# MLP of a two-layer decoder trunk: the first quarter of the first matrix as seven block products too, with its block sums and three token sums on GpSimd

## The chip, the cores and the metric

The kernel runs on one core of one Trainium2 chip. The metric is device time in microseconds (us) of one execution; lower is better. TensorE (PE in the profile) multiplies matrices, VectorE (DVE) and ScalarE (ACT) do elementwise work and read the matmuls' results, GpSimd (POOL) does elementwise work on SBUF and issues some DMAs, and SyncE (SP) issues the other DMAs.

## What is computed

Two layers, each a token mixer (attention and an mLSTM) followed by an MLP. Only the MLP is touched by the change:

```python
u = jax.nn.relu(rmsnorm(x, norm_ffn) @ w_ff1)
return x + (u * u) @ w_ff2
```

x has 512 tokens of 1024 features, w_ff1 is 1024 x 4096, w_ff2 is 4096 x 1024, all float32. The MLP is computed once per layer, so the change acts twice.

## The kernel before, in words

**Numbers in two parts.** TensorE multiplies fp32r numbers. Each float32 operand is split into a high part (`hi`, a copy on ScalarE that rounds) and a low part (`lo`, a subtraction on VectorE of high from the whole). A product of two such operands takes three matmuls (`mm3`, L184): high by high, high by low, low by high. So each block of weights costs one 128x1024 copy on ScalarE (`two_parts`, L1212) and one 128x1024 subtraction on VectorE (L1213) before TensorE can use it. The names are wh and wl for weights, uh and ul for the hidden values, i for the normed tokens, t for sums of them. Four pairs of wh and wl tiles rotate (pool `spl`), so a split also waits until TensorE has finished with the block four halves earlier.

**The four quarters.** w_ff1 is taken in four quarters of 1024 columns (`part` 0 to 3), and w_ff2 in the four matching quarters of 1024 rows. The second matrix (`second_slots`) is done in all quarters as seven block products: a 2x2 block product of matrices with seven instead of eight multiplications, at the price of sums of blocks. The first matrix is done so in quarters 1 to 3 (`first_slots`, L1363). There the tokens' side has four quads: j says which half of the features, t which half of the tokens. The products use quads as they are or sums of quads, t1 to t4, which `t_steps` (L1325) makes once per layer: b12 (whole numbers of one quad), t1 (two sums, in a second scratch tile), t2 (two sums, in place on t1's), t3 (two, in place on b12's), t4 (two, in place on t2's). Each of t1 to t4 is then split in two parts. In before all of these sums are on VectorE (L1332 to L1357). On the weights' side the sums are made by DMAs that add to what is there (`more`, L1382), which GpSimd issues.

**Quarter 0 of the first matrix** is done plainly, by `First` (L1274): four column groups q of 256 columns, each with eight k tiles, two column tiles and three matmuls of 128x512 over all tokens. Groups 0 and 1 run first, woven together, k tiles 4 to 7 before 0 to 3, since the mixer finishes the features of k tiles 4 to 7 first. In between come what `late` holds: the transposes and norm copies (`Norm.turn`, L270: four transposes into an `aux` bank, a copy on ScalarE at L180, an instruction on VectorE at L181) of k tiles 0 to 3. Groups 2 and 3 are the first two `Slot`s.

**The slots.** After that the work is a list of slots of two halves each. `go(i)` prepares the weights up to four halves ahead (`prepare(i + 4)`: loads, splits, sums), then runs half i on TensorE, then reads its banks (`done`). `extra` (L1638) hangs the steps b12, t1, t2, t3, t4 behind halves 1, 3, 5, 9, 13. In quarters 1 to 3, a product of the first matrix is 48 matmuls of 128x256, one of the second matrix 24 of 128x512. The results of a product are first copied from the bank (`first_read`, ScalarE) and later products are added (`then_read`, VectorE, then two activations on ScalarE).

**What sets the order.** The Python order gives each engine's queue a start, but a scheduler reorders within it; what is marked `tc.high_priority()` (loads, weight splits, bank reads) goes ahead of other ready work. `ask` (L1236) makes all loads go out behind the first four. Every engine then runs its own queue strictly in the order that is built, and an instruction that waits holds up those behind it. Raw weight blocks lie in eleven tiles (`raws`) that are handed out in turn; `drop` gives one back.

Of the kernel before, what the change touches and what calls it, by code (L numbers as in the profile page):

```python
# [33 lines left out]
def hybrid_kernel(ctx, tc, x, norm_mix, w_in, att_q_norm, att_k_norm, att_sinks, m_gate_bias,  # L34
# [63 lines left out]
    def f32(ap):  # L98
        return ap.bitcast(F32)
# [1086 lines left out]
    def mlp(l, norm, late, phase):  # L1186
# [24 lines left out]
        def two_parts(src, hi, lo):  # L1211
            sc.activation(hi, src, AF.Copy)  # L1212
            ve.tensor_tensor(lo, src, f32(hi), op=ALU.subtract)  # L1213
            return hi, lo
# [59 lines left out]
        class First:  # L1274


            def __init__(self, q, which="f"):
                self.q, self.which, self.w = q, which, {}

            def load(self, h):  # L1280
                with tc.high_priority():
                    r = raw([P, 4, H])
                    ask(r, w_ff1[l, 4 * h * P:4 * (h + 1) * P, H * self.q:H * (self.q + 1)]
                        .rearrange("(k p) n -> p k n", p=P))
                self.w[h] = w_split(r)
                drop(r)

            def step(self, k, order=range(KT)):
                if k == order[0]:
                    self.ps = banks(self.which)  # L1290
                hi, lo = self.w[k // 4]
                for m in range(2):
                    c = slice(m * P, (m + 1) * P)
                    mm3(self.ps[:, m, :], hi[:, k % 4, c], lo[:, k % 4, c], acts[k][0], acts[k][1],
                        k == order[0], k == order[-1])

            def evac(self, u):
                i, m = self.q // 2, 2 * (self.q % 2)
                with tc.high_priority():
                    for t in range(2):  # L1300
                        dst = u[t, i][:, m:m + 2, :]
                        sc.activation(dst, self.ps[:, :, H * t:H * (t + 1)], AF.Relu)
                        sc.activation(dst, dst, AF.Square)

# [5 lines left out]

        def first_slot(q, u, which):
            f = First(q, which)
            return Slot(f.load, lambda h: [f.step(k) for k in range(4 * h, 4 * h + 4)], lambda: f.evac(u))

# [10 lines left out]
        def t_steps():  # L1325
# [37 lines left out]
        def first_slots(part, new):  # L1363
# [20 lines left out]
            def w2(h):  # L1384
                load(a12, h, 0, 1)

                def then():
                    load(s, h, 1, 0)
                    more(s, h, 1, 1)

                return a12[h], then, a12[h]

            def w1(h):
                load(a11, h, 0, 0)
                return a11[h], lambda: None, a11[h]
# [22 lines left out]
            def fresh_y():  # L1418
                ys[:] = [aux(), aux()]
# [3 lines left out]
            def product_(y, fresh, w, moving, done):  # L1423
# [9 lines left out]
                def run(h):  # L1433
                    if h == 0 and fresh:
                        if y:
                            fresh_y()
# [44 lines left out]
            return {  # L1481
                2: product_(True, True, w2, lambda: quad(1, 0), lambda: first_read((0, 0), True)),
                1: product_(False, True, w1, lambda: quad(0, 0), lambda: then_read((0, 0), False, ALU.add)),
                5: product_(True, True, w5, lambda: t_parts[1], done5),
                6: product_(False, False, w6, lambda: t_parts[2], lambda: first_read((1, 0), False)),
                7: product_(False, False, w7, lambda: t_parts[3], done7),
                3: product_(True, False, w3, lambda: quad(1, 1), lambda: then_read((1, 0), True, ALU.add)),
                4: product_(True, True, w4, lambda: t_parts[4], lambda: then_read((0, 1), True, ALU.add)),
# [131 lines left out]
        f01, turned = [First(0, "f"), First(1, "y")], [4, 5, 6, 7, 0, 1, 2, 3]  # L1620
        for h in (1, 0):
            for f in f01:
                f.load(h)
        weave([(0.5, lambda k=k, f=f: f.step(k, turned)) for k in turned for f in f01], late + [(4.5, factor)])
        for f in f01:
            f.evac(us[0])
        slots = [first_slot(2, us[0], "x"), first_slot(3, us[0], "f")]
        for part in range(4):
            p = second_slots(part, us[part])
            if part < 3:  # L1630
# [100 lines left out]
```

## Time and profile before

| | |
|---|---|
| median of 3 runs | 1270.65 us (1270.12 to 1270.93) |
| profiled execution, span from first to last instruction | 1268.6 us |
| granted TensorE clock | 1.00 throughout |
| busy: PE, DVE, ACT, POOL | 1261.9, 1036.7, 794.4, 265.3 us |
| first matrix starts on TensorE, first and second layer | 317.40 and 946.45 us |

The page of the profile shows one execution. Its sections are: busy time of each engine; the span in 40 slices; DMA queues; the chain of work that ended last, followed back from the end; the costliest groups of instructions; DMA issues. Other views list groups of one stretch, instructions in order of time (start, length, engine, line, operation, output<-input, count), the chain in order of time, and busy time of each engine in given stretches (length, then busy time with the number of instructions for PE, PEld, DVE, ACT, POOL, then the granted clock, the DMA share and GB/s). All times in those views count from the span's start.

### The profile page before, as it was taken

The numbers are of one execution on the slowest core, as the hardware profiler recorded it, in microseconds if no ns is written. First come the engines' busy times: TensorE is split into PE (matmuls) and PEld (weight loads), VectorE is DVE, ScalarE is ACT, GpSimd is POOL, SyncE is SP. The second block draws the span as 40 slices with busy tenths as digits, with TensorE's granted clock in tenths as the row PEclk, the third lists the DMA queues.
The fourth block names the chain that finished last, engine by engine and source line by source line (L and its number), as shares of the span: only waits on it lengthen the run. The fifth ranks groups of instructions, "written<-read, shape, count | busy, mean of one in ns | idle before, by whom it ended". The sixth has DMA issues, their size and how long they took to land.

```text
span 1268.6 us, 19228 instructions
## 1 busy us (share of the span) xinstructions
PE 1261.9 (99%) x6882; PEld 1089.8 (86%) x6882; DVE 1036.7 (82%) x1646; ACT 794.4 (63%) x1403; POOL 265.3 (21%) x361
## 2 busy tenths in 40 slices
PE   9999999999999999999999999999999999999998
PEld 7888888888889999999888888888888899999987
DVE  4788988688787887969957989876878879879697
ACT  5578578546555666656554885876466556565563
POOL 4513131020003031130115041310300121302210
PEclk9999999999999999999999999999999999999999
DMA  5425473476669798897224345634757697988953
GB/s 159 113 71 155 110 123 99 136 141 148 195 156 216 198 200 208 204 205 205 35 75 117 93 124 117 117 112 129 157 136 198 162 220 201 196 218 189 217 143 99
DMA packets 138927, 193.35 MB, mean 152 GB/s; under 512 B 10568, under 2 KB 79024, under 8 KB 138832
## 3 DMA queue, kind: packets, MB, share of 16 engines
q1 hardware_dynamic: 92992, 129.72, 33.3%
q0 software_dynamic: 45120, 62.00, 30.7%
q8 instruction: 54, 0.88, 0.3%
q10 hardware_dynamic: 720, 0.40, 0.1%
q14 instruction: 41, 0.34, 0.1%
HBM read 188.95 MB, written 2.10 MB: 151 GB/s over the span
## 4 chain that ended last, share of the span: by engine, by line
PE 98%; ACT 1%; DVE 0%; issue 0%; DMA 0%; DVEq 0%; POOL 0%; ACTq 0%; POOLq 0%
PE mm L47 79%; PE aux L47 16%; PE aux L52 3%; DMA w<-in_w_in_dram 0%; DVE a L962 0%; ACT wh L167 0%; ACT a L751 0%; ACT L241 0%; ACT L240 0%; ACT a L947 0%; ACT aux L948 0%; ACT t L177 0%; ACT i L180 0%; DVE t L178 0%; ACT kT L598 0%
## 5 line engine op out<-in xcount | busy, mean ns | idle before, releaser
L47 PE MATMUL mm<-i,wh 128*128 128x512 f32 (+1 forms) x1280 | 353.0, 363 | 0.0
L1212 ACT ACTIVATE wh<-raw 128x1024 fp32r<-128x1024 f32 x212 | 223.2, 1056 | 178.9 <-PE mm L47 90.4
L1213 DVE TENSOR_TENSOR wl<-raw,wh 128x1024 fp32r<-128x1024 f32 x212 | 255.4, 1220 | 80.9 <-ACT wh L1212 80.9
L47 PEld LDWEIGHTS mm<-i,wh 128*128 128x128 f32 x1280 | 221.8, 189 | 29.4
L47 PE MATMUL mm<-i,wl 128*128 128x512 f32 (+1 forms) x640 | 229.2, 359 | 0.0
L47 PE MATMUL mm<-wh,uh 128*128 128x512 f32 x440 | 171.8, 390 | 0.0
L47 PE MATMUL mm<-wl,uh 128*128 128x512 f32 x440 | 171.7, 390 | 0.0
L47 PE MATMUL mm<-wh,ul 128*128 128x512 f32 x440 | 171.2, 389 | 0.0
L1382 POOL DMA_DIRECT2D raw<-in_w_ff_dram x48 | 62.6, 1312 | 381.0 <-DMA raw<-in_w_ff_dram 175.6
L47 PEld LDWEIGHTS mm<-i,wl 128*128 128x128 f32 x640 | 120.9, 189 | 18.6
L167 ACT ACTIVATE wh<-w 128x512 fp32r<-128x512 f32 (+1 forms) x144 | 86.3, 603 | 61.6 <-PE mm L47 45.2
L168 DVE TENSOR_TENSOR wl<-w,wh 128x512 fp32r<-128x512 f32 (+1 forms) x144 | 95.6, 667 | 32.9 <-ACT wh L167 31.2
L47 PE MATMUL mm<-wh,i 128*128 128x512 f32 (+1 forms) x352 | 99.5, 356 | 0.6 <-ACT wh L167 0.6
L47 PEld LDWEIGHTS mm<-wh,ul 128*128 128x128 f32 x440 | 82.6, 188 | 17.5
L1267 DVE SCALAR_TENSOR_TENSOR x<-mm,ms,x 128x512 f32<-128x512 f32 x126 | 90.6, 744 | 8.3 <-PE mm L47 8.3
L47 PEld LDWEIGHTS mm<-wh,uh 128*128 128x128 f32 x440 | 82.8, 188 | 16.0
L47 PEld LDWEIGHTS mm<-wl,uh 128*128 128x128 f32 x440 | 82.8, 188 | 15.6
L1539 POOL DMA_DIRECT2D raw<-in_w_ff_dram x36 | 43.5, 1209 | 150.7 <-DVE wl L1213 126.2
L47 PEld LDWEIGHTS mm<-wh,i 128*128 128x128 f32 x352 | 62.0, 188 | 9.4 <-ACT wh L167 0.8
L47 PE MATMUL aux<-t,wh 128*128 128x256 f32 x384 | 69.5, 283 | 0.0
L47 PE MATMUL aux<-i,wh 128*128 128x256 f32 x384 | 69.5, 283 | 0.0
L47 PE MATMUL mm<-wl,i 128*128 128x512 f32 (+1 forms) x176 | 61.8, 351 | 0.0
(324 smaller groups left out, 2531.8 us busy)
## 6 DMA issues: line engine op xcount, KB each, us to landing
raw<-in_w_ff_dram SPq DMA_DIRECT2D x144, 512.0 KB, 4.9
raw<-in_w_ff_dram POOLq DMA_DIRECT2D x84, 512.0 KB, 8.1
w<-in_w_in_dram SPq DMA_DIRECT2D x112, 256.0 KB, 2.7
a<-in_w_in_dram POOLq DMA_DIRECT2D x32, 256.0 KB, 5.8
qa<-in_w_out_dram POOLq DMA_DIRECT2D x12, 512.0 KB, 6.6
a<-in_w_in_dram SPq DMA_DIRECT2D x16, 256.0 KB, 4.4
w<-in_w_att_branch_dram SPq DMA_DIRECT2D x16, 256.0 KB, 2.9
w<-in_w_m_branch_dram SPq DMA_DIRECT2D x16, 256.0 KB, 2.9
```

The source lines that it names most:

```text
L47: latest[0] = nc.tensor.matmul(*args, **kw)
L52: latest[0] = nc.tensor.transpose(*args)
L167: sc.activation(wh[:, :off], raw[:, :off], AF.Copy)
L168: ve.tensor_tensor(wl[:, :off], raw[:, :off], f32(wh[:, :off]), op=ALU.subtract)
L1212: sc.activation(hi, src, AF.Copy)
L1213: ve.tensor_tensor(lo, src, f32(hi), op=ALU.subtract)
L1267: ve.scalar_tensor_tensor(xh[:, cc], ps[i][:, cc], ms[j][:, b:b + 1], xh[:, cc], op0=ALU.mult, op1=ALU.add)
L1382: gp.dma_start(to[h], src(h, i, j), accum_op=ALU.add)
L1539: gp.dma_start(to[h], src(h, i, j), accum_op=ALU.add)
```

## The change

`First` and `first_slot` go. Quarter 0 becomes seven block products too, and these are the order of the slots now: product 2 of quarter 0, product 2 of quarter 1, then products 1, 5, 6, 7, 3, 4 of quarter 0, then the second matrix of quarter 0 mixed with the rest of quarter 1. In quarter 0 the sums of weight blocks are not made by adding DMAs: four blocks are loaded for each half (a11, a12, b10, b11; one more, a22, later), and GpSimd adds them in place, four sums of 128x1024 for each half: b11 += b10, b10 += a11, a11 += b11, a12 += a11. In the token sums, the two additions each of t2, t3 and t4 go from VectorE to GpSimd. These are plain two-operand sums, so t2 and t4 are made with the other sign, and the split turns it (`minus=True`: scale -1 on ScalarE, a scalar_tensor_tensor on VectorE). b12 and t1 stay on VectorE, and so do all splits. The steps hang behind halves 3 (b12 and t1), 5, 7 and 9 (`sums_at`). The norm copies that `late` holds now come behind halves 0 to 2 (one half counts 1.0), at 1.0, 1.5, 2.0 and 2.5.

```diff
+        def two_parts(src, hi, lo, minus=False):
+            if minus:
+                sc.activation(hi, src, AF.Copy, scale=-1.0)
+                ve.scalar_tensor_tensor(lo, src, -1.0, f32(hi), op0=ALU.mult, op1=ALU.subtract)
...
-        class First:
...
             def t2():
                 d = scratch["b"]
-                ve.scalar_tensor_tensor(d, d, -1.0, h22, op0=ALU.mult, op1=ALU.subtract)
-                ve.tensor_tensor(d, d, l22, op=ALU.subtract)
-                t_parts[2] = two_parts(d, *t_new("t2"))
+                gp.tensor_tensor(d, d, h22, op=ALU.add)
+                gp.tensor_tensor(d, d, l22, op=ALU.add)
+                t_parts[2] = two_parts(d, *t_new("t2"), True)
             def t3():
                 d = scratch["a"]
-                ve.tensor_tensor(d, h22, d, op=ALU.subtract)
-                ve.tensor_tensor(d, d, l22, op=ALU.add)
+                gp.tensor_tensor(d, h22, d, op=ALU.subtract)
+                gp.tensor_tensor(d, d, l22, op=ALU.add)
                 t_parts[3] = two_parts(d, *quad(0, 1))
             def t4():
                 d = scratch["b"]
-                ve.tensor_tensor(d, d, h21, op=ALU.add)
-                ve.tensor_tensor(d, d, l21, op=ALU.add)
-                t_parts[4] = two_parts(d, *t_new("t4"))
+                gp.tensor_tensor(d, d, h21, op=ALU.subtract)
+                gp.tensor_tensor(d, d, l21, op=ALU.subtract)
+                t_parts[4] = two_parts(d, *t_new("t4"), True)
...
+            if part == 0:
+                b10, b11 = ([None] * 2 for _ in range(2))
+                def add(to, h, more_):
+                    with tc.high_priority():
+                        gp.tensor_tensor(to[h], to[h], more_[h], op=ALU.add)
+                def begin(h):
+                    load(b10, h, 1, 0)
+                    load(b11, h, 1, 1)
+                def w2(h):
+                    load(a12, h, 0, 1)
+                    return a12[h], lambda: None
+                def w1(h):
+                    load(a11, h, 0, 0)
+                    def then():
+                        add(b11, h, b10)
+                        add(b10, h, a11)
+                        add(a11, h, b11)
+                    return a11[h], then
+                def w5(h):
+                    return b11[h], lambda: None, b11[h]
+                def w6(h):
+                    return a11[h], lambda: add(a12, h, a11), a11[h]
+                def w7(h):
+                    return b10[h], lambda: None, b10[h]
+                def w3(h):
+                    return a12[h], lambda: None, a12[h]
...
-        f01, turned = [First(0, "f"), First(1, "y")], [4, 5, 6, 7, 0, 1, 2, 3]
...
-        slots = [first_slot(2, us[0], "x"), first_slot(3, us[0], "f")]
+        begin0, f0 = first_slots(0, us[0], {2: "y", 5: "y"})
+        f1 = first_slots(1, us[1], {2: "x"}, begin0)[1]
+        slots = [f0[2], f1[2]] + [f0[n] for n in (1, 5, 6, 7, 3, 4)]
...
-        extra = dict(zip((1, 3, 5, 9, 13), t_steps()))
+        sums_at, sums = {3: 2, 5: 1, 7: 1, 9: 1}, []
...
-        weave(steps, side)
+        weave([(1.0, go) for _, go in steps[:5]], late + [(4.0, factor)])
+        weave(steps[5:], side)
...
-        late = norm.steps(0, 1.5, 0.5)
+        late = norm.steps(0, 1.0, 0.5)
```

The lines of the changed program are 2 to 4 off from those of before (L1212 is L1216, L1213 is L1217). The names in the rows below, for the first layer: i_3583, i_3584 are the high and low parts of the normed tokens of k tiles 4 to 7, i_3765, i_3766 (before: i_3748, i_3749) those of k tiles 0 to 3; raw_3895 (before: raw_3969) is the scratch tile of b12 and t3, raw_3897 (before: raw_4046) that of t1, t2 and t4; t_829, t_830 (before: t_849, t_850) are the two parts of t1. Of the weights, raw_3703 and raw_3709 are a12 of quarter 0 (halves 0 and 1), raw_3725 is the second half of a12 of quarter 1, raw_3721 and raw_3731 are b10, raw_3723 and raw_3733 b11, raw_3769 and raw_3819 a11. aux_3853 (before: aux_3784) is the bank with the last of the four transposes that `late` holds.

VectorE at the start of the MLP, before: the low parts of four weight blocks are done, then come the norm copies, b12, and the low part of a block of column group 2.

```order
L1213 TENSOR_TENSOR wl_3720<-raw_3717,wh_3719 128x1024
L181 SCALAR_TENSOR_TENSOR i_3749<-aux_3743,gcol,i_3748 128x512
L181 SCALAR_TENSOR_TENSOR i_3749<-aux_3758,gcol,i_3748 128x512
L181 SCALAR_TENSOR_TENSOR i_3749<-aux_3771,gcol,i_3748 128x512
L181 SCALAR_TENSOR_TENSOR i_3749<-aux_3784,gcol,i_3748 128x512
L1332 TENSOR_TENSOR raw_3969<-i_3748,i_3749 128x1024
L1213 TENSOR_TENSOR wl_3886<-raw_3883,wh_3885 128x1024
```

And now, at the same place, three blocks ahead of the norm copies and five behind:

```order
L1217 TENSOR_TENSOR wl_3718<-raw_3715,wh_3717 128x1024
L181 SCALAR_TENSOR_TENSOR i_3766<-aux_3760,gcol,i_3765 128x512
L181 SCALAR_TENSOR_TENSOR i_3766<-aux_3805,gcol,i_3765 128x512
L181 SCALAR_TENSOR_TENSOR i_3766<-aux_3812,gcol,i_3765 128x512
L181 SCALAR_TENSOR_TENSOR i_3766<-aux_3853,gcol,i_3765 128x512
L1300 TENSOR_TENSOR raw_3895<-i_3765,i_3766 128x1024
L1217 TENSOR_TENSOR wl_3728<-raw_3725,wh_3727 128x1024
L1217 TENSOR_TENSOR wl_3772<-raw_3769,wh_3771 128x1024
L1217 TENSOR_TENSOR wl_3822<-raw_3819,wh_3821 128x1024
L1217 TENSOR_TENSOR wl_3865<-raw_3723,wh_3864 128x1024
```

The fourth weight block that TensorE needs (wl_3728, second product, second half) moved behind the norm copies and b12; in before the fourth (wl_3720) stood ahead of them.

ScalarE, some way on, before: the high part of t1 (t_849) between weight splits.

```order
L1212 ACTIVATE wh_3891<-raw_3889 128x1024
L240 ACTIVATE nrt_3817<-nv_3813 128x4
L1212 ACTIVATE t_849_4049<-raw_4046 128x1024
L241 ACTIVATE ncol_3816<-nrt_3817 128x4
L1212 ACTIVATE wh_3897<-raw_3895 128x1024
```

And now:

```order
L1216 ACTIVATE wh_3920<-raw_3733 128x1024
L1466 ACTIVATE u_3892<-mm_3828 128x512 x2
L262 ACTIVATE junk,nss_3147<-x_0_89 128x512
L1216 ACTIVATE wh_3949<-raw_3769 128x1024
L1216 ACTIVATE i_3765<-raw_3895 128x4x256
L1216 ACTIVATE t_829_3900<-raw_3897 128x1024
L1216 ACTIVATE wh_3987<-raw_3819 128x1024
```

The high part of t3 (written to i_3765 from raw_3895) moved to the place right before that of t1; in before it stands some twenty rows behind it.

GpSimd, before: the adding DMAs of the mixer's end, and right behind them those of the MLP's weights.

```order
L1145 DMA x_0_87<-st_3365 128x512
L1105 DMA t_3247<-in_w_out_dram 128x512
L1105 DMA t_3262<-in_w_out_dram 128x512
L1382 DMA raw_4015<-in_w_ff_dram 128x4x256
L1382 DMA raw_4059<-in_w_ff_dram 128x4x256
```

And now, from the last of the mixer's DMAs to the second sum of t3:

```order
L1105 DMA t_3262<-in_w_out_dram 128x512
L1390 TENSOR_TENSOR raw_3723<-raw_3723,raw_3721 128x1024
L1390 TENSOR_TENSOR raw_3721<-raw_3721,raw_3769 128x1024
L1390 TENSOR_TENSOR raw_3733<-raw_3733,raw_3731 128x1024
L1390 TENSOR_TENSOR raw_3731<-raw_3731,raw_3819 128x1024
L1390 TENSOR_TENSOR raw_3769<-raw_3769,raw_3723 128x1024
L1390 TENSOR_TENSOR raw_3703<-raw_3703,raw_3769 128x1024
L1390 TENSOR_TENSOR raw_3819<-raw_3819,raw_3733 128x1024
L1390 TENSOR_TENSOR raw_3709<-raw_3709,raw_3819 128x1024
L1317 TENSOR_TENSOR raw_3895<-i_3583,raw_3895 128x1024
L1318 TENSOR_TENSOR raw_3895<-raw_3895,i_3584 128x1024
```

Eight block sums and the two of t3 moved in; the two of t2 and the two of t4 follow, and then the adding DMAs. The second layer has the same rows in the same order.

More of the change, by code (lines that the diff above doesn't have):

```diff
@@ L1385, in w2 @@
                 load(a12, h, 0, 1)
[L1387 to L1391, printed above, removed]
+                return a12[h], lambda: (after_two or begin)(h), a12[h]
+            def begin(h):
+                load(s, h, 1, 0)
+                more(s, h, 1, 1)
             def w1(h):
                 load(a11, h, 0, 0)
-                return a11[h], lambda: None, a11[h]
+                return a11[h], lambda: after_two and begin(h), a11[h]
             def w5(h):
```

76 lines of the change are left out of this document (23 added, 53 removed).

## The prediction

> **What bounds the kernel now.** I read the page first: how busy each engine is, and who owns the chain of work that ended last.
>
> ```profile
> span 1268.6 us, 19228 instructions
> PE 1261.9 (99%) x6882; PEld 1089.8 (86%) x6882; DVE 1036.7 (82%) x1646; ACT 794.4 (63%) x1403; POOL 265.3 (21%) x361
> PE 98%; ACT 1%; DVE 0%; issue 0%; DMA 0%; DVEq 0%; POOL 0%; ACTq 0%; POOLq 0%
> ```
>
> TensorE owns 98% of the chain, so a matmul saved is time saved, and any wait on TensorE is time lost. Next come the chain in order of time around the start of the first MLP and at the same place in the second layer, and engine time by stretch.
>
> ```profile
> 316.64 0.77 PE aux L52 x6
> 317.40 4.10 PE mm L47 x18
> ...
> 326.34 0.44 PE aux L52 x4
> 326.77 40.84 PE mm L47 x180
> 367.62 5.75 PE aux L47 x48
> ...
> 955.80 40.84 PE mm L47 x180
> 996.64 5.75 PE aux L47 x48
> ```
>
> ```profile
> 306.70:367.60 60.90, 60.90 (x286) 50.30 (x284) 44.68 (x52) 38.23 (x62) 2.58 (x2) 1.00 0.63 181
> 367.60:631.00 263.40, 263.40 (x1637) 238.48 (x1636) 224.36 (x225) 159.59 (x164) 53.23 (x44) 1.00 0.81 181
> ```
>
> The MLP's matmuls start at 317.40 and TensorE never waits until 631. VectorE (third pair of numbers in the last two rows) is at 44.68 of 60.90 us in the stage that changes, GpSimd (fifth) at 2.58. Both layers show the same pieces, so I work out the first and double it.
>
> **TensorE's own work.** A 512-wide matmul costs 40.84/180 = 0.2269 us, a 256-wide one 5.75/48 = 0.1198. Per layer the change removes 4 x 8 x 2 x 3 = 192 of the first (43.56 us) and adds 7 x 48 = 336 of the second (40.25). It saves 3.3 us per layer, 6.6 in all, if nothing waits. The transposes stay. I number the new half products 0 to 15 (24 matmuls, 2.88 us each): 0 and 1 are the first quarter's product 2, 2 and 3 the second quarter's, then products 1 (4, 5), 5 (6, 7), 6 (8, 9), 7, 3 and 4.
>
> **Price of GpSimd's sums.** Before has no 128x1024 sum there. The nearest rows are four 128x512 sums in a stretch, in each layer, what VectorE did just before and meanwhile (in order of time), and a smaller product from the groups.
>
> ```profile
> 31.36 4.12 POOL L515 TENSOR_TENSOR t<-a 128x512 f32<-128x512 f32 x4 [7.82 <-ACT a L416]
> 660.19 4.43 POOL L515 TENSOR_TENSOR t<-a 128x512 f32<-128x512 f32 x4 [32.12 <-ACT a L416]
> ```
>
> ```profile
> 30.72 0.86 DVE L304 TENSOR_SCALAR t<-ident,nch 128x128 fp32r<-128x128 f32 x4
> 31.50 4.06 DVE L304 TENSOR_SCALAR t<-ident,ncl 128x128 fp32r<-128x128 f32 x4
> ...
> 659.13 0.43 DVE L168 TENSOR_TENSOR wl<-w,wh 128x264 fp32r<-128x264 f32 x1 [2.29 <-ACT wh L167]
> 661.85 0.67 DVE L168 TENSOR_TENSOR wl<-w,wh 128x264 fp32r<-128x264 f32 x1 [2.29 <-ACT wh L167]
> ```
>
> ```profile
> L547 POOL TENSOR_TENSOR rp<-a,ct 128x128 f32<-128x128 f32 x8 | 3.8, 477 | 0.0
> ```
>
> 4.12/4 = 1.03 us for half the size, so I take 2.06 for 128x1024. Bounds: 2.22 by the second row (4.43/4, doubled); below, a line through 128x128 at 0.477 and 128x512 at 1.03 adds 0.74 for 512 more, 1.77. The same rows show that the two engines exclude each other: four small VectorE instructions took 0.86 us alone and 4.06 beside GpSimd, one per GpSimd sum, and a 128x264 subtraction, two SBUF inputs like those here, took 0.67 instead of 0.43, in the middle of GpSimd's stretch. The rule in the Trainium skill, SBUF — State Buffer, "SBUF: two separate sides", is that a VectorE instruction with two SBUF inputs and a GpSimd one that reads SBUF take a shared port pair in turn, each for its whole length. By that rule, and these rows agree, the sums below are those with turns (27.5 us per layer), without it those without (18.4).
>
> The Trainium skill, GPSIMD Engine Reference, "Elementwise — side-by-side cycle accounting", has 4497 ns for 2048 fp32; half, an estimate, is 2.25, by which ten sums in the chain below would add 1.9 us per layer.
>
> **Moved on ACT and VectorE: half 3.** Here the order of the built program decides. ScalarE's split of the second quarter's second half (wh_3727) stands behind the last of the four norm copies (from aux_3853), whose transposes are issued right before half 3. VectorE then has its part of that copy, the token sum b12, and only then wl_3728 and wl_3772. In before the same four instructions stand in that order, with timings:
>
> ```profile
> 326.81 0.69 ACT L180 ACTIVATE i<-aux,gcol 128x512 fp32r<-128x512 f32 x1 [1.15 <-PE aux L52]
> ```
>
> ```profile
> 327.53 0.75 DVE L181 SCALAR_TENSOR_TENSOR i<-aux,gcol,i 128x512 fp32r<-128x512 f32 x1 [1.08 <-ACT i L180]
> 328.32 1.22 DVE L1332 TENSOR_TENSOR raw<-i,i 128x1024 f32<-128x1024 f32 x1
> 329.46 1.22 DVE L1213 TENSOR_TENSOR wl<-raw,wh 128x1024 fp32r<-128x1024 f32 x1
> ```
>
> There no matmul was behind that split. Now half 3 is. TensorE reaches it at 317.40 + 3 x 2.88 + 10 transposes x 0.11 (0.44/4) = 327.1; ScalarE's copy ends 0.69 later, at 327.8 instead of 327.5; so wl_3728 begins at 329.8 and ends at 331.0, and wl_3772, 1.14 behind it (328.32 to 329.46), ends at 332.15. Of half 3 and 4 four matmuls (0.48) can run ahead. **A** = 331.0 - 327.1 - 0.5 = 3.4 us. It already eats the saving. The weights are there: the loads begin to go out at 310.31, and six go out 0.46 apart, and the slowest of that time landed 13.2 us after its issue, which makes 325.8 for the last.
>
> ```profile
> 310.31 0.92 SPq L1239 DMA_DIRECT2D raw<-in_w_ff_dram  x2
> ```
>
> ```profile
> DMA to landing us min/median/max: 3.5/4.8/13.2
> ```
>
> **GpSimd's queue: half 6.** Halves 3 to 5 then end at 331.0 + 68 x 0.1198 = 339.15. Half 6 (product 5) moves t1, whose parts are t_829 on ScalarE and t_830 on VectorE. t1 is summed on VectorE as before, but ScalarE's queue has the copy of t3 (i_3765 from raw_3895) in front of t_829, and t3 is now summed on GpSimd, behind all eight block sums. The fifth block sum writes raw_3769 in place, which wl_3772 reads until 332.15. From there six GpSimd instructions must pass: four block sums and t3's two, 6 x 2.06 = 12.4 us, to 344.5. Queued behind t3's copy on ScalarE are t_829 and wh_3987; on VectorE wl_3988 stands in front of t_830. Three ScalarE copies in a row take 2.94, two VectorE instructions 1.14 + 1.22:
>
> ```profile
> 315.46 2.94 ACT L1212 ACTIVATE wh<-raw 128x1024 fp32r<-128x1024 f32 x3
> ```
>
> ```profile
> L1302 ACT ACTIVATE u<-mm 128x512 f32<-128x512 f32 x8 | 4.5, 586 | 0.0
> ```
>
> 344.5 + 5.3 = 349.8: **B** = 10.7 us without turns. In the same stretch VectorE has six instructions with two SBUF inputs ready (wl_3822, wl_3865, t1's two sums, wl_3921, wl_3950). If each goes ahead of one GpSimd sum, 6 x 1.14 = 6.8 us come on top: 356.65, B = 17.5.
>
> **Halves 8 and 12.** t2 is summed in place in t1's buffer, so it starts when t_830 has read it, at the moment that half 6 gets going: two sums 4.12, ScalarE 1.05 (one 128x1024 copy), VectorE 1.22 = 6.4, against 5.75 of halves 6 and 7. **C** = 0.6; one VectorE turn more (1.14) makes 1.8. t4 follows in the same buffer behind t_843, and TensorE's order has 17 matmuls of half 12 behind half 9. They need wh_4080, which ScalarE has behind t4's copy, wh_4052 and two bank reads (0.59 each), and wl_4081: 4.12 + 2.94 + 1.17 + 1.22 = 9.45 against 5.75. **D** = 3.7, with a turn 4.8. Behind that, nothing: GpSimd has only the DMA sums left, which are read some ten half products later; SP's next loads wait until GpSimd has read the blocks that they overwrite, but serve half 15 and later; the six VectorE instructions that left for GpSimd (6 x 1.22) pay for the six added weight splits; the bank sums (four of 1.2 us) come late and TensorE is not waiting for them.
>
> Sum per layer: with turns 3.4 + 17.5 + 1.8 + 4.8 = 27.5, less 3.3, is 24.2; without turns 3.4 + 10.7 + 0.6 + 3.7 = 18.4, less 3.3, is 15.1. Twice 24.2 is 48.4: the profiled span would be 1317.0. The median of the runs is 1270.65, 2.05 above the profiled span, all of it outside the span as far as the trace tells; I add the same: **1319 us**. Without turns it is 1300.9.
>
> A clock term is left. TensorE's last work lies before 1266, and the granted clock dips after it; at the start matmuls took 660 ns that take 283 later:
>
> ```profile
> 1264.00:1266.00 2.00, 0.90 (x4) 0.40 (x3) 1.21 (x3) 0.00 (x0) 0.00 (x0) 1.00 0.34 131
> 1266.00:1268.60 2.60, 0.00 (x0) 0.00 (x0) 0.00 (x0) 0.00 (x0) 0.00 (x0) 0.91 0.29 101
> ```
>
> ```profile
> L47 PE MATMUL aux<-ones 128*128 128x256 f32 x6 | 2.9, 660 | 1.2 <-POOL ones L109 1.2
> L47 PE MATMUL aux<-i,wh 128*128 128x256 f32 x384 | 69.5, 283 | 0.0
> ```
>
> So a wait as long as B restarts TensorE slowly: six matmuls at 0.38 more are 2.3 us. After B this is covered, since C and D hang on GpSimd's chain; after D it is not. I put it at nothing for the forecast and at 2.3 per layer for the upper end.
>
> **Rivals.** First, no turns: GpSimd and VectorE run side by side, because VectorE's instructions are queued at other moments than I think. Against it stand 4.06 for 0.86 and 0.67 for 0.43; for it, that VectorE, when it waits for ScalarE, leaves gaps. 1301 us. Second, and on the other side: the sums stay covered and TensorE remains the bound, 1270.65 - 6.6 = 1264.0. It decides by GpSimd's price p: 332.15 + 6p + 5.3 must not pass 339.15, so p has to be 0.3 us or less, where a sum of half the size took 1.03; and A must go as well, which it would if ScalarE's copy for half 3 were taken in front of the norm copy. For it speaks only that GpSimd has 2.58 of 60.90 us busy there. Third, the same covered sums but with A in place: 2 x (3.4 - 3.3) = +0.2, 1270.9, no change.
>
> **How the numbers follow.** With turns, 0.62, 1319 us; without, 0.25; covered and faster 0.04; covered with A 0.03; slower than all this 0.06. Lower end: the cheapest sum (1.77) without turns makes B 8.9; with C and D gone, A + B - 3.3 = 9.0, twice that is 18.0, 1289. Upper end: the forecast plus 2 x 2.3 for the clock and ten sums at 2.22 (2 x 1.6), 1327; a us for rounding, 1328. That leaves out little over 1 in 10. 0.2% (2.5 us) is about what a measurement of this kernel can tell from no change: faster 0.04, same 0.03, slower 0.93.
>
> **What would show it.** In the changed profile: TensorE waits for VectorE's wl just before half 3 (about 3 us) and for a t part before half 6 (10 to 18 us), in each layer, and ScalarE waits for GpSimd at the copy of t3; a 128x1024 GpSimd sum takes 1.8 to 2.2 us; subtractions beside them are stretched beyond 1.22. TensorE's matmul time falls by 6 to 7 us. I am wrong if TensorE doesn't wait at half 6, if GpSimd's sums take well under 1 us, or if the loss lies elsewhere, among the later quarters.

## The result, and the profile after

| | before | after |
|---|---|---|
| median of the runs | 1270.79 us (1270.12 to 1271.74, 4 runs) | 1335.65 us (1333.71 to 1337.15, 4 runs) |
| profiled execution, span | 1268.6 us | 1333.9 us |
| mean granted TensorE clock | 1.00 | 0.98 |

The ratio is 1.0508, 95% interval 1.0494 to 1.0523. The change costs 65 us. The prediction had the direction and most of the mechanism, but 1319 us was 17 us too low, and its range ended at 1328.

First the head of the page of after: the span, and busy time of each engine.

```profile
span 1333.9 us, 19860 instructions
PE 1273.0 (95%) x7170; PEld 1112.1 (83%) x7170; DVE 1090.9 (82%) x1658; ACT 813.8 (61%) x1411; POOL 352.0 (26%) x389
```

TensorE was to be 6.6 us less busy and is 11.1 us busier (1261.9 before): some of its matmuls run slowly. Next what TensorE waited for in after (total, times, longest; twice means once per layer).

```profile
PE mm L47 <- ACT t L1216: 26.3, 2, 13.1
PE mm L47 <- ACT wh L1216: 12.2, 6, 3.9
PE mm L47 <- DVE t L1217: 6.3, 2, 3.1
PE aux L52 <- DVE x L1138: 3.3, 2, 1.7
PE mm L47 <- DVE wl L1217: 2.5, 4, 0.8
PE aux L52 <- DVE i L181: 2.0, 2, 1.0
...
PE mm L47 <- DVE t L1214: 0.8, 2, 0.4
```

Half the sum is 26.7 us per layer. The prediction had 27.5 for A to D; A to D alone measure 24, and the rest are waits that it did not have. The first and third rows are B, the wait ahead of half 6 for the two parts of t1: 16.3 us (17.5 predicted). The second and the fifth hold A and D (3.9 + 0.5). The rows with L52 (2.7 us per layer) are new: TensorE waits ahead of transposes, before half 3 is reached. Now GpSimd in after, in order of time.

```profile
314.65 2.41 POOL L1390 TENSOR_TENSOR raw<-raw,raw 128x1024 f32<-128x1024 f32 x1 [23.41 <-DMA raw<-in_w_ff_dram]
318.73 9.06 POOL L1390 TENSOR_TENSOR raw<-raw,raw 128x1024 f32<-128x1024 f32 x3 [1.67 <-DMA raw<-in_w_ff_dram]
335.35 13.24 POOL L1390 TENSOR_TENSOR raw<-raw,raw 128x1024 f32<-128x1024 f32 x4 [7.56 <-DVE wl L1217]
348.56 3.32 POOL L1317 TENSOR_TENSOR raw<-i,raw 128x1024 f32<-128x1024 f32 x1
351.95 3.20 POOL L1318 TENSOR_TENSOR raw<-raw,i 128x1024 f32<-128x1024 f32 x1
```

And VectorE beside it in the same form, at the start, before half 6, and where t1's low part is made; behind it ScalarE at the end of the wait of half 6.

```profile
315.09 3.05 DVE L1217 TENSOR_TENSOR wl<-raw,wh 128x1024 fp32r<-128x1024 f32 x1 [2.18 <-ACT wh L1216]
318.06 1.27 DVE L1138 TENSOR_TENSOR x<-x,mm 128x512 f32<-128x512 f32 x2
319.26 6.29 DVE L1217 TENSOR_TENSOR wl<-raw,wh 128x1024 fp32r<-128x1024 f32 x2
...
346.32 3.35 DVE L1305 TENSOR_TENSOR raw<-raw,i 128x1024 f32<-128x1024 f32 x1
349.60 3.36 DVE L1217 TENSOR_TENSOR wl<-raw,wh 128x1024 fp32r<-128x1024 f32 x1
352.88 2.29 DVE L288 TENSOR_TENSOR nv<-nss 128x4 f32<-128x4 f32 x1
...
359.68 1.22 DVE L1217 TENSOR_TENSOR t<-raw,t 128x1024 fp32r<-128x1024 f32 x1
```

```profile
355.18 1.06 ACT L1216 ACTIVATE i<-raw 128x1024 fp32r<-128x1024 f32 x1 [12.92 <-POOL raw L1318]
356.15 1.04 ACT L1216 ACTIVATE t<-raw 128x1024 fp32r<-128x1024 f32 x1
```

The turns are there as forecast: from 335.35 to 355.15 six GpSimd sums take 19.8 us, 3.3 each, with one VectorE instruction between any two, shown with 3.4 us since its wait counts as busy. So is ScalarE's queue: 12.92 us of waiting for t3's sum, and only then t1's copy, though t1's own sums ended on VectorE at 346.32 + 3.35 = 349.7. What the prediction did not have is the upper half: the first four sums take turns too, with the first weight splits (3.05 and 6.29/2 = 3.1 us for 1.22), and the bank sums of x that the transposes read stand behind those. In before the same VectorE instructions ran without turns:

```profile
314.98 1.23 DVE L1213 TENSOR_TENSOR wl<-raw,wh 128x1024 fp32r<-128x1024 f32 x1 [2.17 <-ACT wh L1212]
316.12 1.28 DVE L1138 TENSOR_TENSOR x<-x,mm 128x512 f32<-128x512 f32 x2
```

And TensorE in after: the transposes (L52) that wait, and half 3.

```profile
316.57 0.49 PE L52 MATMUL aux<-ident,x 128*128 128x128 f32 x3
318.79 0.55 PE L52 MATMUL aux<-ident,x 128*128 128x128 f32 x3 [1.74 <-DVE x L1138]
...
326.26 0.65 PE L52 MATMUL aux<-ident,x 128*128 128x128 f32 x4 [0.96 <-DVE i L181]
...
331.96 0.50 PE L47 MATMUL mm<-i,wh 128*128 128x256 f32 x2 [1.72 <-ACT wh L1216]
```

Last, the granted clock (the column before the DMA share) in stretches of layer 1 of after: halves 3 to 5, the wait, its end, halves 6 and 7, half 8 and 9, the wait D, and the next four halves.

```profile
334.20:344.20 10.00, 9.90 (x68) 9.70 (x68) 10.00 (x5) 6.30 (x13) 8.77 (x3) 0.83 0.35 105
344.20:357.20 13.00, 0.00 (x0) 0.00 (x0) 11.90 (x5) 2.02 (x3) 10.79 (x4) 0.64 0.28 81
357.20:361.00 3.80, 0.63 (x2) 0.34 (x2) 3.78 (x5) 3.21 (x4) 0.00 (x0) 0.50 0.53 142
361.00:368.80 7.80, 7.74 (x48) 7.53 (x48) 6.58 (x8) 3.21 (x5) 5.64 (x2) 0.74 0.22 67
368.80:375.10 6.30, 5.90 (x47) 5.70 (x47) 1.44 (x2) 0.09 (x1) 5.72 (x2) 1.00 0.25 83
375.10:380.20 5.10, 0.79 (x2) 0.50 (x2) 3.60 (x4) 5.10 (x7) 0.00 (x0) 0.85 0.30 88
380.20:394.10 13.90, 13.86 (x96) 13.86 (x97) 6.04 (x6) 5.49 (x7) 2.60 (x2) 0.81 1.02 235
```

After each wait TensorE runs for some microseconds at half rate. 48 matmuls take 7.74 instead of 48 x 0.1198 = 5.75, and the 96 behind D take 13.86 instead of 11.50: 2.0 and 2.4 us. Halves 3 to 5 take 9.90 instead of 68 x 0.1198 = 8.15, another 1.7.

### The profile page after: what moved, and what is told of

It is laid out like the page before. It is cut to its first block, busy times and chain, and to the rows that moved or that the text cites. A ratio compares the mean times of both kernels' runs of the same rounds, so it can differ in the third digit from the quotient of the medians.

```text
span 1333.9 us, 19860 instructions
## 1 busy us (share of the span) xinstructions
PE 1273.0 (95%) x7170; PEld 1112.1 (83%) x7170; DVE 1090.9 (82%) x1658; ACT 813.8 (61%) x1411; POOL 352.0 (26%) x389
## 5 line engine op out<-in xcount | busy, mean ns | idle before, releaser
L1217 DVE TENSOR_TENSOR wl<-raw,wh 128x1024 fp32r<-128x1024 f32 x224 | 293.2, 1327 | 77.5 <-ACT wh L1216 77.4
L47 PE MATMUL mm<-i,wh 128*128 128x256 f32 (+1 forms) x1344 | 340.0, 345 | 12.2 <-ACT wh L1216 12.2
L1216 ACT ACTIVATE wh<-raw 128x1024 fp32r<-128x1024 f32 x224 | 234.5, 1054 | 165.0 <-PE mm L47 81.2
L47 PEld LDWEIGHTS mm<-i,wh 128*128 128x128 f32 x1344 | 230.7, 196 | 33.2 <-ACT wh L1216 13.5
L47 PE MATMUL mm<-i,wl 128*128 128x256 f32 (+1 forms) x672 | 227.9, 341 | 2.5 <-DVE wl L1217 2.5
L47 PEld LDWEIGHTS mm<-i,wl 128*128 128x128 f32 x672 | 130.8, 195 | 16.9 <-DVE wl L1217 3.5
L47 PE MATMUL mm<-t,wh 128*128 128x256 f32 x320 | 63.0, 297 | 33.3 <-ACT t L1216 26.3
L47 PEld LDWEIGHTS mm<-t,wh 128*128 128x128 f32 x320 | 53.7, 203 | 35.2 <-ACT t L1216 26.7
L47 PE MATMUL aux<-t,wh 128*128 128x256 f32 x448 | 81.5, 283 | 0.0
L47 PEld LDWEIGHTS aux<-t,wh 128*128 128x128 f32 x448 | 70.6, 192 | 0.9
```

Of the source, the lines that this page charges most:

```text
L47: latest[0] = nc.tensor.matmul(*args, **kw)
```

## The experiments

Two theories stood at the beginning. One: the loss is all as predicted, and what is missing is the clock, some 6 us per layer. The rival: the sums on GpSimd do more damage than the sum counted, in places that it did not look at.

### Where GpSimd's sums cost

Four kernels put some of the sums elsewhere or in another order, and a fifth takes four of them away. In the first the additions of t2, t3 and t4 are on VectorE again, as in the kernel before, with the split without the sign. In the second the block sums are on VectorE, and in the third both. The edit of the second:

```diff
                 def add(to, h, more_):
                     with tc.high_priority():
-                        gp.tensor_tensor(to[h], to[h], more_[h], op=ALU.add)
+                        ve.tensor_tensor(to[h], to[h], more_[h], op=ALU.add)
```

> Only change: the six token sums of t2, t3 and t4 go back to VectorE as in the kernel before; the block sums stay on GpSimd. Theory (t3 behind eight GpSimd block sums holds ScalarE's copy for t1, and that is most of B): half 6's wait falls from 16.3 to about 8 us and half 12's from 4.4 to about 1, the sums on VectorE give back some 5 us at half 8 and by t1's own rest being later, half rate about 5 us per layer: 1310 to 1320 us. Rival (the wait of half 6 is set by the turns between GpSimd's block sums and VectorE's weight splits, and t3 is not to blame): half 6's wait stays over 13 us, 1330 to 1338 us.

Measured: 1319.67 us (1315.29 to 1322.01), ratio to before 1.0379 (1.0358 to 1.0401). As the theory had it: half 6 waits 5.8 + 0.7 us in layer 1 and 8.2 + 0.7 in layer 2, half 12 no more, half 8 5.3.

> Only change: the six block sums go to VectorE; the six token sums stay on GpSimd. Theory (each two-input sum on GpSimd takes a turn of VectorE, about 2.1 us, against 1.2 us for the sum on VectorE itself): the 2.7 us of waits ahead of half 3 go, half 6's wait falls to about 9 us since t3 no longer stands behind the block sums, half 8 about 2.7, half 12 about 4.9, half rate 5 to 6 us per layer: 1308 to 1318 us. Rival (VectorE is the engine in short supply, and GpSimd's sums relieve it): VectorE's splits come later, the waits of halves 3 to 8 grow, 1336 to 1345 us.

Measured: 1315.61 us (1312.97 to 1316.01), ratio 1.0347 (1.0332 to 1.0363). The time is in the theory's range, the waits are others: those at the transposes go, half 6 waits 4.2 us, half 12 3.8, and one that no theory had stands in half 4, 4.4 us for the last norm copy (L181), which VectorE now has behind the block sums.

> Only change: all twelve sums on VectorE, none on GpSimd; blocks as seven products and the order of the slots as in the kernel after. Theory (the sums on GpSimd cost more than they relieve): no turns, half 3 about 2.6 us, half 6 about 8.5, half 8 about 4.7, half 12 about 2, half rate about 5 us per layer: 1303 to 1313 us. Rival (GpSimd relieves VectorE as the change means it to): 1336 us or over. If it is under 1271 us, the sums' place was the whole of the loss, and the order of the slots costs nothing.

Measured: 1303.9 us (1303.7 to 1304.4), ratio 1.0261 (1.0244 to 1.0278). Also in the theory's range, but not by its waits: half 6 waits 1.0 us where it had 8.5, and 5.9 us for the last norm copy stand in half 4, so the agreement is in part luck. Of the 65 us, 32 come from having the sums on GpSimd rather than on VectorE, which they were to relieve. The rest is still there with no sum on GpSimd.

In the fourth only ScalarE's and VectorE's splits of t1 and t3 change places:

```diff
+                t1_two[:] = last_two
...
-                t_parts[3] = two_parts(d, *quad(0, 1))
+                with tc.issue_after(t1_two[0].ins), tc.issue_after(t1_two[1].ins):
+                    t_parts[3] = two_parts(d, *quad(0, 1))
```

> Only change: ScalarE's and VectorE's split of t3 is issued behind that of t1. All sums stay where the kernel after has them. Theory (t3, summed on GpSimd behind all block sums, stands in ScalarE's queue ahead of t1's copy, and the chain from t1 to t2 and t4 sets the waits behind it): t1's copy runs when t1's sums are done (about 350 instead of 356 us), half 6's waits fall by 4 to 6 us, and t2 follows earlier by as much, so that little of it comes back at half 8: 4 to 6 us per layer, 1323 to 1328 us. Rival (the turns on VectorE alone set t1's parts): half 6 begins earlier but its second operand comes as late as before, 1333 to 1337 us.

Measured: 1326.01 us (1324.55 to 1328.33), ratio 1.0435 (1.0421 to 1.0449), 9.6 us less than after. From the profile of this run, ScalarE, then VectorE:

```profile
350.21 1.06 ACT L1218 ACTIVATE t<-raw 128x1024 fp32r<-128x1024 f32 x1 [6.50 <-DVE raw L1307]
355.70 1.06 ACT L1218 ACTIVATE i<-raw 128x1024 fp32r<-128x1024 f32 x1 [4.43 <-POOL raw L1321]
```

```profile
350.10 3.37 DVE L1219 TENSOR_TENSOR wl<-raw,wh 128x1024 fp32r<-128x1024 f32 x1
353.39 2.29 DVE L288 TENSOR_TENSOR nv<-nss 128x4 f32<-128x4 f32 x1
355.61 1.21 DVE L1219 TENSOR_TENSOR t<-raw,t 128x1024 fp32r<-128x1024 f32 x1
```

t1's copy now waits for t1's own sum only. Half 6's wait is 10.8 us instead of 16.3: some 5 us of B were t3's place in the queue. The rest is the turns: t1's low part still stands behind a split and a tiny instruction that each wait for a GpSimd sum.

Then only the first four sums, those from 314.65 on:

```diff
                 def begin(h):
                     load(b10, h, 1, 0)
                     load(b11, h, 1, 1)
+                    more(b11, h, 1, 0)
+                    more(b10, h, 0, 0)
...
                     def then():
-                        add(b11, h, b10)
-                        add(b10, h, a11)
                         add(a11, h, b11)
```

> Only change: the first four block sums on GpSimd (those that ran from 314.65 on, beside the first weight splits) are made by adding DMAs; the other four block sums and six token sums stay on GpSimd. Theory (these four sums take turns with the first splits, so TensorE reaches half 3 some 3 us late, and since the fifth sum waits for the split of half 4 the delay goes through GpSimd's whole chain to the end): the two waits ahead of half 3 (1.7 and 1.0 us) go, the fifth sum starts about 332 instead of 335.35, 2.7 to 3.2 us per layer, 1329 to 1331 us. Rival (the chain from half 3 on has slack for it, B shrinks or grows to the same end): 1334 to 1337 us.

Measured: 1330.67 us (1329.24 to 1332.32), ratio 1.0471 (1.0455 to 1.0487), 5.0 us less than after. GpSimd and VectorE of this run:

```profile
333.32 13.26 POOL L1390 TENSOR_TENSOR raw<-raw,raw 128x1024 f32<-128x1024 f32 x4 [8.09 <-DVE wl L1217]
```

```profile
316.06 1.22 DVE L1217 TENSOR_TENSOR wl<-raw,wh 128x1024 fp32r<-128x1024 f32 x1 [2.17 <-ACT wh L1216]
317.20 1.28 DVE L1138 TENSOR_TENSOR x<-x,mm 128x512 f32<-128x512 f32 x2
318.39 2.36 DVE L1217 TENSOR_TENSOR wl<-raw,wh 128x1024 fp32r<-128x1024 f32 x2
```

TensorE of this run:

```profile
317.55 0.93 PE L52 MATMUL aux<-ident,x 128*128 128x128 f32 x6
...
329.91 0.50 PE L47 MATMUL mm<-i,wh 128*128 128x256 f32 x2 [1.72 <-ACT wh L1216]
```

The splits are back at 1.22 us and no transpose waits. From the first transposes to half 3 TensorE needs 329.91 - 1.72 - 317.55 = 10.6 us, where after needs 331.96 - 1.72 - 316.57 = 13.7: the four sums cost 3.0 us, in the second layer as in the first. GpSimd's later chain starts only 2.0 us earlier (333.32 instead of 335.35), since in this execution the mixer ended 1.0 us later. The difference reaches the end: the medians differ by 2.5 us per layer.

### The clock

> Only change: TensorE gets unneeded 128x512 matmuls (fp32r, results never read) in the waits of both layers: 7 ahead of half 3, 56 ahead of half 6 and 13 behind half 6's first matmul, 16 behind half 9. The sums stay where they are. Theory (the clock term was mis-sized: after each wait TensorE runs at half rate, about 7 us per layer): the waits for data stay about as long, but the half-rate stretches at 334-338, 348-365 and 379-385 us mostly go, 5 to 7 us per layer less: 1321 to 1326 us. Rival 1 (the matmuls behind the waits are slow because of the shared port or of their operands, not because TensorE had stood still): the half-rate stretches stay, no gain, 1334 to 1340 us. Rival 2 (the filling only moves the time): the waits shrink, but half 6 starts later by what the filling overruns, 1330 to 1340 us.

```diff
+        def filler(idle, count):
+            with tc.issue_after(latest[0].ins):
+                for _ in range(count):
+                    g = norm.groups[1][0]
+                    pe.matmul(idle[:, 0, :], g[:, 0, 0:P], g[:, 0, :], start=True, stop=True)
```

Measured: 1334.27 us (1333.65 to 1336.17), ratio 1.0501 (1.0485 to 1.0517): no gain, at a mean clock of 0.996 instead of 0.98. The theory as I put it fell, and so did the reason of the first rival, since the half rate did go. Stretches of this run, from half 6 on:

```profile
361.00:369.00 8.00, 6.33 (x49) 5.87 (x48) 6.75 (x10) 2.68 (x5) 5.67 (x2) 1.00 0.24 70
369.00:377.00 8.00, 7.37 (x48) 7.37 (x49) 1.96 (x3) 2.47 (x3) 4.76 (x2) 0.79 0.01 2
...
381.00:393.00 12.00, 11.68 (x97) 11.69 (x98) 5.78 (x6) 6.24 (x7) 2.60 (x2) 1.00 1.07 261
```

Halves 6 and 7 run at full rate and end at 367.3, then half 8 waits for t2, whose low part ends at 369.6 (369.1 in after). So a slow half 6 had cost nothing. The last row is what D's half rate is worth: the same 12 us hold 97 matmuls at full rate, where after needs 13.86 for 96. But the filling behind half 9 ended at 380.7 and half 10 then waited for a bank read, so that gain was spent. Two runs take the waits apart:

> Only change: 56 unneeded 128x512 matmuls ahead of half 6 and 13 behind its first matmul (results never read). Theory (halves 6 and 7 run faster by 1.9 us, but half 8 then waits for t2, whose GpSimd sums start when t1 has been read, whatever TensorE does): the half-rate stretch at 348 to 365 us goes, the wait ahead of half 8 grows by what half 6 gains, no change, 1333.5 to 1336.5 us. Rival (every half-rate stretch reaches the end): 1.9 us per layer or more, 1330 to 1332 us.

Measured: 1336.79 us (1336.21 to 1337.27), ratio 1.0516 (1.0502 to 1.053): no gain, 1.1 us above after and 0.3 above the theory's range. The clock is at 1.00 from 357.2 to 369; half 8 waits 1.1 + 0.9 us for t2's parts instead of 0.4, runs slowly in its turn, and D follows with its half rate. The mechanism is as the theory said: the chain from t1 over GpSimd to t2 sets half 8.

> Only change: 8 unneeded 128x512 matmuls (results never read) behind half 9, in the last of the long waits (3.9 us, ahead of half 12). Theory (of the half-rate stretches only the last reaches the end, since behind it nothing is late; it costs 2.4 to 3 us per layer): most of that stretch goes, 2 to 2.8 us per layer, 1330 to 1332 us. Rival (the filling of all waits took under a us per layer off, so the clock costs nothing here either): 1334 to 1337 us.

Measured: 1337.15 us (1333.39 to 1338.28), ratio 1.0516 (1.0501 to 1.053), above both ranges, the rival's by 0.15. This run can't decide. With 8 matmuls put in, only 2 of half 12's matmuls instead of 17 stand ahead of half 10, which then waits 1.4 us for the reading of its bank, and the half rate is only shortened. What D costs had to be asked without filling: take the wait away.

```diff
             def t4():
-                gp.tensor_tensor(d, d, h21, op=ALU.subtract)
-                gp.tensor_tensor(d, d, l21, op=ALU.subtract)
-                t_parts[4] = two_parts(d, *t_new("t4"), True)
+                ve.tensor_tensor(d, d, h21, op=ALU.add)
+                ve.tensor_tensor(d, d, l21, op=ALU.add)
+                t_parts[4] = two_parts(d, *t_new("t4"))
```

(t2 still has the other sign here, so this t4 is another sum; number, kind and size of the instructions are those of before.)

> Only change: t4's two sums go back to VectorE; all other sums stay on GpSimd. t4 is the last link of the chain, nothing is late behind it. Theory with the clock (the wait of 3.9 us ahead of half 12 costs its own length and 2.4 us of half rate behind it): the wait falls to about 1 us and the half-rate stretch behind it goes, 5.5 to 6.5 us per layer, 1322.5 to 1325 us. Rival (only the wait counts): 3 to 3.9 us per layer, 1328 to 1330 us.

Measured: 1324.66 us (1323.65 to 1325.95), ratio 1.0424 (1.0408 to 1.0439): 11.0 us less than after, 5.5 per layer. The wait at that place falls from 3.9 + 0.5 to 0.9 us; the next 96 matmuls in this run:

```profile
375.90:387.40 11.50, 11.50 (x96) 11.50 (x97) 5.94 (x6) 5.59 (x7) 2.60 (x2) 1.00 1.04 239
```

3.5 us of waiting and 13.86 - 11.50 = 2.4 us of half rate make 5.9, near the 5.5 measured; the wait alone does not.

### What is left without GpSimd's sums

With all sums on VectorE 33 us were left. Four kernels ask whether the seven products in front cost that by themselves. The first uses the adding DMAs of the other quarters for quarter 0 as well, with all token sums on VectorE (the branch `if part == 0` of `first_slots` goes).

> The first quarter's block sums are made by adding DMAs, as the other quarters have them, and all token sums are on VectorE; GpSimd sums nothing. Theory (it is the sums' place, not the order of the slots, that costs): no turns, so half 3 about 2.6 us and half 6 1 to 3; the adding DMAs in a chain (6 to 10 us each from issue to landing) make half 8 wait 5 to 8 us; half rate 2 to 3; 1285 to 1298 us. Rival (two quarters' products in front leave too little time for any way of summing): as with all sums on VectorE, 1302 to 1310 us.

Measured: 1301.79 us (1300.71 to 1308.61), ratio 1.0254 (1.0232 to 1.0275). Above the theory's range, and 0.2 us below the rival's. In the profiled execution (1308.61 us) half 8 of layer 1 waits 8.4 us and half 3 waits 4.3. Half 3's load now goes out eleventh and lands at 329.6 (332.9 is the load behind it), and ScalarE copies it at 330.46, behind three pieces of the next norm. The rival's time fits better. Its reason is not shown: VectorE has 17 us less to do here than in the kernel with all sums on it (1061.9 instead of 1078.5 us busy), and the next three kernels are faster with the same two quarters in front.

```diff
-        slots = [f0[2], f1[2]] + [f0[n] for n in (1, 5, 6, 7, 3, 4)]
+        p0 = second_slots(0, us[0])
+        slots = [f0[2], f1[2], f0[1], f0[5], p0[1]] + [f0[n] for n in (6, 7, 3, 4)]
```

> The kernel with the first quarter's block sums by adding DMAs and all token sums on VectorE, and one more edit: the first product of the second matrix (10.9 us of matmuls that need neither token sums nor block sums of the first quarter) comes ahead of product 6. Theory (with nothing on GpSimd the loss is want of other work while sums are made): the waits of 8.4 us ahead of half 8 go with their half rate, half 3's 4.3 us stay; 1279 to 1290 us. Rival (VectorE is full in this stage, so the wait only moves ahead of the product that was pulled forward): 1296 to 1304 us.

Measured: 1286.98 us (1285.89 to 1288.92), ratio 1.0128 (1.0113 to 1.0144). In the theory's range. Half 8's wait is gone; 2.0 us stand ahead of the product that was pulled forward, 3.8 at half 3.

```diff
-            if len(first_asked) < 4:
+            if len(first_asked) < 8:
```

> As the kernel before it in this list, and the first eight weight loads of each MLP go out in the order in which they are used, so that half 3's load, which went out eleventh and landed at 332.9, lands by about 326. Theory: half 3's 4.3 us go as well, 1270 to 1280 us, about as before. Rival (the splits that now stand ahead of the norm copies wait for their loads and hold those): the wait moves from half 3 to the transposes or half 4, 1279 to 1290 us.

Measured: 1292.2 us (1289.85 to 1292.51), ratio 1.0162 (1.0145 to 1.0179). Half 3 no longer waits, but the sum is worse than either number: the wait moved, and to another place than the rival said. VectorE of this run:

```profile
341.15 1.23 DVE L1253 TENSOR_TENSOR raw<-raw,raw 128x1024 f32<-128x1024 f32 x1 [3.31 <-DMA raw<-in_w_ff_dram]
342.29 1.22 DVE L1217 TENSOR_TENSOR wl<-raw,wh 128x1024 fp32r<-128x1024 f32 x1
343.43 1.22 DVE L1217 TENSOR_TENSOR t<-raw,t 128x1024 fp32r<-128x1024 f32 x1
```

t1's low part stands behind a block sum of the second matrix that waits 3.3 us for a load, and that nobody needs for a long time. That order was changed next:

```diff
+                        with tc.issue_after(t1_two[1].ins):
                             ve.tensor_tensor(dst, dst, ps, op=op)
...
+                with tc.issue_after(t1_two[1].ins) if h else ExitStack():
                     ws.append(w_split(r))
...
+                if part == 0:
+                    return qa[h], lambda: None
...
+                if part == 0:
+                    ve.tensor_tensor(qa[h], qa[h], b12[h], op=ALU.add)
+                    drop(b12[h])
```

> The kernel with adding DMAs, the second matrix's first product pulled forward and the loads in order, and one more edit: VectorE takes t1's split ahead of the bank sum and the second weight split of the product that was pulled forward, and that product's two block sums, which nobody needs for 40 us, come later. Theory (with GpSimd's sums gone, what is left of the loss is t1's place in VectorE's queue, behind a sum that waited for its load until 341): the waits of 7.1 us ahead of half 6 and of the pulled product shrink to 1 to 3 with their 2 us of half rate, 6.5 to 8.5 us per layer, 1275 to 1279 us. Rival (VectorE has too little time in this stage in any order): the waits come back at half 8 or 12, 1285 to 1293 us.

Measured: 1275.8 us (1275.08 to 1277.09), ratio 1.0042 (1.0028 to 1.0056), at a clock of 1.00 and in the theory's range. The waits of TensorE:

```profile
PE mm L47 <- DVE t L1219: 2.4, 4, 0.9
PE mm L47 <- DVE wl L1219: 1.4, 4, 0.4
...
PE mm L47 <- ACT t L1218: 1.1, 2, 0.5
PE mm L47 <- DVE ul L1219: 1.0, 2, 0.5
...
```

So the seven products in front need not cost the time. With the block sums made by DMAs, one product of the second matrix between and t1's split first, 5 us of the 65 are left. The product pulled forward was worth 15 us, the order of the sums and splits on VectorE 16; what that order would be worth with the sums on GpSimd was not run. But none of these kernels beats the one before: what is left are many waits of under a microsecond, 2.9 us of them in the first MLP, and they use up the saving. In this profile the two MLPs take 1.2 and 1.5 us longer than in before and the mixer between them 2.1; why the mixer does stays open.

## Why the prediction was right and where it failed

**Right: the direction, the turns, and half 6.** Six GpSimd sums behind the split of half 4 took 19.8 us where the sum had 19.2, and all of B measured 16.3 where it had 17.5; with the 1.7 us that the slow halves 3 to 5 took out of this wait, 18.0. t3's copy ahead of t1's was worth 5 us of it (the run with t1 first). The rest goes with the sums on GpSimd and their turns: without any of them half 6 waits 1.0 us. GpSimd's price was bounded at 1.77 to 2.22 us, with an estimate of 2.25 beside it; alone a sum takes 2.41, above all of these. The sum in turns went by 2.06 + 1.14 = 3.20 where 3.3 was measured.

**Right in size: A, C and D.** A is 1.7 + 0.45 + 0.8 = 2.96 (3.4 predicted), D 3.9 + 0.5 = 4.4 (4.8). C is 0.4 us of waiting, where 1.8 were predicted, but halves 6 and 7 themselves took 2.0 longer; from t1's low part to t2's it took 8.2 us where the sum had 7.6.

**Failed: "TensorE reaches it at 317.40 + 3 x 2.88 + 10 transposes x 0.11 (0.44/4) = 327.1".** TensorE was free for half 3 at 331.96 - 1.72 = 330.24, 3.1 us later. I had counted turns only from the fifth block sum on and took the first four for free, since GpSimd had little to do there. But they meet VectorE's first splits, and the bank sums that the transposes need stand behind those. Since the fifth sum waits for the split of half 4, all of the 3.1 goes on to the end. The run with these four sums as DMAs shows that they are the cause: without them the stretch from the first transposes to half 3 takes 10.6 us, as in this sum (327.1 less 316.5, the start of these transposes in before), and with them 13.7. So the arithmetic held, and what it had at nothing is 3.0 us per layer in the trace and 2.5 in the time of the runs.

**Failed: "I put it at nothing for the forecast and at 2.3 per layer for the upper end".** The clock. The reasoning in front of that choice was right: behind B it is covered (e7_fill_six), behind D it is not. So the forecast should have had it. It measures 2.4 us per layer, nearly what the upper end allowed, but that the sizes agree is luck. The 2.3 came from six matmuls at the start of the kernel, where the granted clock read 1.00; here it stood at 0.50 from 378.7 to 385.4, and some 25 matmuls came 0.21 us apart instead of 0.12.

**The ledger.** The span is 65.3 us longer, 32.6 per layer, where the forecast had 24.2. Of the 8.4 us, 3.1 are half 3's late start, 2.4 the clock behind D, and 2.2 small excesses along the chain (six sums 0.6, the way to t1's low part 0.45, t2 0.65, D's chain 0.5). TensorE also enters the second layer with a wait of 0.8 us that before does not have, half of which counts here. That makes 8.1. The range ended at 1328 because it had room for the clock but none for a start that is later than the arithmetic said.

**Not as stated: the saving.** The sum had 6.6 us less of matmuls. In the only run at a full clock (e13_sums_behind) TensorE is busy 1260.0 us against 1261.9, 1.9 less. The matmuls' own price was right: without a wait, the way to half 3 took the 10.6 us of the sum. The matmuls around each short wait are drawn out (0.38 us for the first one behind a wait, where others are shown with 0.28), which is part of the difference; no run here separates the rest.

**The rivals.** Without turns (1301): refuted, the rows show them. Covered sums (1264 or 1271): a sum would have had to take 0.3 us; it takes 2.4 to 3.3.

## What to carry to other kernels

Work is relieved from an engine only if it does not come back as waiting on the same engine: here a sum of two operands moved to GpSimd held VectorE for about 2.1 us (3.3 for one instruction in turns, less its own 1.2), where VectorE needs 1.2 us to do it itself. In a sum over waits, ask of each delay whether the next operand is late anyway; the last wait of a chain has nothing behind it and carries its half-rate matmuls in full. And when work is moved to the front of a stage, check the first instructions of that stage for the same contention that is counted further on.

## What the runs showed of the hardware

- A 128x1024 sum on GpSimd took 2.41 us alone and 3.2 to 3.4 in turns; VectorE's split, 1.22 alone, is shown with 3.1 to 3.4 beside it. A small VectorE instruction waits as long: one of 128x4 (L288) took 2.29 us at 352.88, and the same instruction takes 0.15 in before.
- The granted clock went to 0.50 after each wait of 3 us and more in one piece, and also in e1_filler behind two waits of 1.1 and 0.9 us with one matmul between (0.79 on the mean of 369 to 377). The length alone did not decide: A's three pieces (1.7, 0.45 and 0.8 us) were followed by 0.50 in both layers of after, but in e7_fill_six only in the second layer, and a wait of 2.1 us ahead of half 6 in e1_filler left 1.00 in the first layer and not in the second. The Trainium skill, TensorE: Matmul & The Clock Gate, "Part 1: The HAM clock gate", has the half rate after at least one idle window of about 3.4 us. Here 2 us of waiting within some 2.4 us were enough in one place, and in the first layer of e1_filler the waits of half 6 and half 12, filled with unneeded matmuls, kept 1.00.
- Taking such waits away by filling them did not make the kernel faster in any of three runs. Ahead of half 8 the next operand came no earlier (e1_filler, e7_fill_six); ahead of half 10 the filling itself put a wait for a bank in (0.6 us in e1_filler, 1.4 in e6_fill_last).
